# Hybrid attention and recurrence layer on one Trainium2 core: the value projections taken first, from x without its norm, and the rest of the order around them

## Chip, core and metric

One core of one Trainium2 chip runs the kernel. The metric is the device time of one execution in microseconds (us). The kernel before was run three times: 492.39, 494.06 and 495.75 us, a median of 494.06 us.

## The reference, cut to what matters

One layer, 512 tokens, model width 1024, all in float32:

```python
xn = rmsnorm(h, norm_gain)
aq, ak, av, ag, bq, bf, bi, bg, gate_a, gate_b = split(xn @ w_in)
qa, ka, va = rmsnorm(heads(aq)), rmsnorm(heads(ak)), heads(av)      # 8 heads x 64
ya = (causal_attention(qa, ka, va, rel_bias) * silu(ag)) @ w_up_a
log_f, kb, qb, vb = gates(bf), (1 - lb) * sigmoid(-bf), silu(bq), bi # 4 heads x 128
yb = (rmsnorm(hgrn2(qb, kb, vb, log_f)) * silu(bg)) @ w_up_b
h = h + (sigmoid(gate_a) * ya + sigmoid(gate_b) * yb) @ w_out
out = h + (p @ w_ple) * sigmoid(h @ w_ple_gate)
```

The norm of x is one factor per token (1/rms) and one per channel (the gain). A projection whose output has a token on each partition can therefore be made from x times the gain alone, and the factor per token multiplied in when the result is taken out of PSUM.

## The kernel before, in words

Every float32 product is made of three matmuls on rounded parts: high x high, high x low, low x high. A weight tile comes by DMA into a raw tile (two buffers), ScalarE (ACT) rounds it to its high part `wh`, VectorE (DVE) subtracts to get the low part `wl` (`split`, L181; three buffers of each). `weight` (L238) asks for the tile two places ahead, so that `wh` and `wl` of tile i+2 are made while TensorE (PE) works on tile i; the slot that they need is that of tile i-1, and comes free when the last matmul on that tile is done.

PE's order is written by hand: a manual schedule runs instructions in the order in which the code emits them. The main line emits projections and, after every three matmuls or so, adds their length to a clock of its own (`tick`, L120). Side jobs (generators given to `spawn`, L99) say how long they want to wait and emit their next piece once that clock has reached the time. The order on the other engines comes from the scheduler, which places instructions by readiness in its own timeline and by priority: code under `tc.high_priority` is preferred.

The main line: `bi` (the recurrence's values) from `gh`, `gl` (x times the gain, L282); the sum of squares of x on ACT, GpSimd (POOL) and DVE while that runs (`x_squares`, L292); `x_normalise` (L307) makes 1/rms with two small matmuls `mp` and `mt` and then `xh`, `xl`, the normalised x. From these come `bf` and `bq` of the four recurrence heads (each followed by `hgrn_gates`, L422), then `aq`, `ak`, `av`, and then the list `ORDER` (L43): the silu projections `bg` and `ag`, the merge gates `gb` and `ga`, and the up-projections `ub` of the recurrence between them. After the list come `ua`, `h` (w_out) and `g` (w_ple_gate, with `pe` for w_ple).

Side jobs: `recurrence` (L590) for four heads, whose pieces `HP` = 3.2 us apart make ratio tiles `hx` on DVE and ACT, score matmuls `lpb` and `lpa`, then `hktp`, `hds`, `hop` and `hms`; it starts `H0` = 23.85 us after the first head's gates. `qk_norm` (L601) for q and k ends in the transposes `qtp`, `ktp`. `attention` (L631) has 16 steps (4 head pairs, 4 query blocks): scores `s` on PE, then on DVE and ACT the softmax `p` (add the bias and find the maximum, L649; exp, L651; reciprocal; scale, L653), then transposes `pt` on PE, and `o` (times the values) once per head pair. A step is `AP` = 6.0 us of the main line's clock: 0.7 of it lies between scores and transposes of the same step.

`hgrn_gates` of a head: ACT makes `ha` = log(1 + exp(-|bf|)) in three passes and `hu` in two, DVE makes `hu`, `ha`, `hk`, POOL adds `ha` and `hu` (L435), and DVE scans that sum in four pieces (L439); then come the sigmoid of `bq` and the product with it.

Of the kernel before, what the change touches and what calls it, by code (L numbers as in the profile page):

```python
# [15 lines left out]
OP = mybir.AluOpType  # L16
# [14 lines left out]
HP = 3.2  # L31
AP = 6.0
H0 = 23.85
XN = 1.45
# [8 lines left out]
ORDER = [("bg", 0), ("ag", 0), ("bg", 1), ("ag", 1), ("gb", 0), ("gb", 1), ("bg", 2), ("ag", 2), ("gb", 2), ("gb", 3),  # L43
         ("bg", 3), ("ag", 3)] + [("gb", i) for i in range(4, 8)] + [("ga", 4), ("ga", 5), ("ga", 6), ("ub", 0), ("ub", 1)]
ORDER += [("ga", 7), ("ub", 2), ("ub", 3), ("ga", 0), ("ub", 4), ("ub", 5), ("ga", 1), ("ub", 6), ("ub", 7), ("ga", 2),
          ("ga", 3)]
# [7 lines left out]
def hybrid_layer_kernel(  # L54
# [136 lines left out]
    def w_sequence():  # L191
        for kp in range(4):
            wseq.append((w_tok[2, kp], 2, 512))
        for i in range(GH):
            wseq.append((w_tr[i], KD, 128))
            wseq.append((w_tr[4 + i], KD, 128))
        for g in (0, 1):
            for kp in range(4):
                wseq.append((w_tok[g, kp], 2, 512))
        for kp in range(4):  # L200
            wseq.append((w_tok[3, kp], 2, 512))
# [100 lines left out]
    def x_norm():
        with tc.high_priority():
            x_normalise()
        yield 0.0

    def x_normalise():  # L307
        ssum = ssums[1]
        V.tensor_tensor(ssum, ssum, ssums[0], op=OP.add)
# [28 lines left out]
        rsqrt(rt, tt, mt[:, 0:NT])  # L338

# [22 lines left out]
    def proj_tr(i, name):  # L362
        ws = weight(w_tr[i])
        ps = bank("mm", name)
        mm3(ps, ws[0], ws[1], xh, xl, KD)
        return ps

    def proj_pair(ids, names):

        ws = [weight(w_tr[i]) for i in ids]  # L370
        ps = [bank("mm", n) for n in names]
        for k in range(KD):
            for p, (wh, wl) in zip(ps, ws):
                for j, (a, b) in enumerate(((wh, xh), (wh, xl), (wl, xh))):
                    PE.matmul(p, a[:, k, :], b[k], start=(k == 0 and j == 0), stop=(k == KD - 1 and j == 2))
            tick(1.362)
        return ps
# [253 lines left out]
    def attention(qn, kn, va, sags, res):  # L631
# [57 lines left out]

        steps = [(hp, qb) for hp in range(HPAIRS) for qb in range(NT)]  # L690
# [31 lines left out]
    def start(kp):  # L722
        with tc.high_priority():
# [9 lines left out]
            elif kp == 1:  # L733
# [15 lines left out]
    lower_bound()
    spawn(recurrence(vb, sbgs, yb))  # L750
    for i in range(GH):
        if i == 0:
            f_, q_ = proj_pair((0, 4), ("bf0", "bq0"))
        else:
            f_ = proj_tr(i, f"bf{i}")
            q_ = proj_tr(4 + i, f"bq{i}")
# [151 lines left out]
```

## Time and profile before

| what | us |
|---|---|
| median of three runs | 494.06 |
| the profiled execution, device time | 494.47 |
| its span, first to last instruction | 492.5 |
| PE busy | 476.8 (97%) |
| DVE busy | 302.0 (61%) |
| ACT busy | 261.8 (53%) |
| POOL busy | 37.4 (8%) |

How to read the rows below: a timeline row is start, length, engine, line, operation, output <- inputs, shapes and count; behind it in brackets the idle time of the engine just before, and what ended it. Matmuls overlap: a 512-column matmul shows 0.39 us, but the next starts 0.227 us after it, so that an idle time of PE in brackets is some 0.16 us less than the time that PE lost there.

### The profile page before, as it was taken

Reading aid. Unit: us, or ns where it says so; the run is one execution under the profiler, and the core shown is the slowest. Engines: PE = TensorE matmul, PEld = TensorE weight load, DVE = VectorE, ACT = ScalarE, POOL = GpSimd, SP = SyncE. Lnnn points to the kernel's source line nnn. Section 1 sums busy time; section 2 is a strip of 40 time slices with the busy share of each in tenths; the row PEclk is TensorE's granted clock in tenths of the full one; section 3 lists DMA queues with packets and bytes.
Section 4 is the critical chain, followed back from the end, with each engine's and each line's share of the span. In section 5 each row is a group of like instructions: output and inputs, shape, how many; then the busy total and the mean of one; then the engine's idle time right before and its main releaser. Section 6 shows DMA issues by size and latency. Waiting matters only on the chain.

```text
span 492.5 us, 7947 instructions
## 1 busy us (share of the span) xinstructions
PE 476.8 (97%) x3160; PEld 387.2 (79%) x3160; DVE 302.0 (61%) x592; ACT 261.8 (53%) x458; POOL 37.4 (8%) x46
## 2 busy tenths in 40 slices
PE   7889999999999997999999999999999999999996
PEld 6668887888788776787777787888888888888885
DVE  3897886668985888359666544333327955534332
ACT  6665867535545777468685656644334533233111
POOL 3230221050401000010001000000000000000000
PEclk9999999999999999999999999999999999999999
DMA  8331332521231323113212222423323554323211
GB/s 276 128 120 66 110 128 88 149 87 45 63 94 60 91 82 115 58 44 94 79 44 99 75 64 91 130 81 95 119 64 87 192 191 129 108 85 128 87 43 43
DMA packets 17797, 48.41 MB, mean 98 GB/s; under 512 B 2232, under 2 KB 2616, under 8 KB 17760
## 3 DMA queue, kind: packets, MB, share of 16 engines
q1 hardware_dynamic: 17616, 47.83, 30.1%
q8 instruction: 24, 0.39, 0.3%
q0 software_dynamic: 144, 0.09, 0.1%
q14 instruction: 13, 0.11, 0.1%
HBM read 45.79 MB, written 2.12 MB: 97 GB/s over the span
## 4 chain that ended last, share of the span: by engine, by line
PE 88%; DVE 6%; DMA 2%; issue 2%; ACT 1%; SPq 0%; DVEq 0%; ACTq 0%
PE ga L251 9%; PE g L251 9%; PE h L251 9%; PE gb L251 8%; PE bg L251 5%; PE aq L399 5%; PE ak L399 4%; PE ub L251 4%; PE ua L251 4%; PE av L399 4%; PE ag L251 4%; PE bq L251 3%; PE bf L251 3%; PE pe L251 2%; PE s L642 2%; PE o L679 2%
## 5 line engine op out<-in xcount | busy, mean ns | idle before, releaser
L183 DVE TENSOR_TENSOR wl<-wf,wh 128x1024 fp32r<-128x1024 f32 (+1 forms) x81 | 92.3, 1141 | 85.8 <-ACT wh L182 85.5
L182 ACT ACTIVATE wh<-wf 128x1024 fp32r<-128x1024 f32 (+1 forms) x81 | 78.0, 963 | 122.9 <-PE ga L251 26.6
L251 PE MATMUL gb<-xh,wh 128*128 128x512 f32 x64 | 27.5, 429 | 0.0
L251 PE MATMUL g<-hl,wh 128*128 128x512 f32 (+1 forms) x72 | 26.3, 365 | 0.0
L251 PE MATMUL g<-hh,wl 128*128 128x512 f32 (+1 forms) x72 | 26.3, 365 | 0.0
L251 PE MATMUL g<-hh,wh 128*128 128x512 f32 (+1 forms) x72 | 26.3, 365 | 0.0
L651 ACT ACTIVATE p<-p,ps 128x128 f32<-128x128 f32 (+3 forms) x32 | 17.8, 556 | 15.0 <-DVE ps L649 14.9
L251 PE MATMUL gb<-xh,wl 128*128 128x512 f32 x64 | 25.4, 397 | 0.1
L251 PE MATMUL gb<-xl,wh 128*128 128x512 f32 x64 | 25.5, 398 | 0.0
L251 PE MATMUL ga<-xh,wh 128*128 128x512 f32 x64 | 25.3, 396 | 0.0
L251 PE MATMUL ga<-xl,wh 128*128 128x512 f32 x64 | 24.9, 389 | 0.0
L251 PE MATMUL ga<-xh,wl 128*128 128x512 f32 x64 | 24.9, 389 | 0.0
L251 PE MATMUL h<-ml,wh 128*128 128x512 f32 x64 | 24.9, 389 | 0.0
L251 PE MATMUL h<-mh,wl 128*128 128x512 f32 x64 | 24.9, 389 | 0.0
L251 PE MATMUL h<-mh,wh 128*128 128x512 f32 x64 | 24.9, 389 | 0.0
L649 DVE CUSTOM_DVE_ANT_0 p<-s,bias 128x128 f32<-128x128 f32 (+3 forms) x32 | 14.7, 488 | 15.7 <-PE s L642 15.7
L461 ACT ACTIVATE hx<-hx 128x512 f32<-128x512 f32 x24 | 14.9, 630 | 7.6 <-DVE hx L460 7.3
L530 POOL COPY sc<-s 32x128 f32<-32x128 f32 x16 | 8.7, 544 | 128.5 <-DVE s L481 127.9
L663 PE MATMUL pt<-ident,p 128*128 128x128 f32 x80 | 12.4, 287 | 5.0 <-DVE p L653 5.0
L667 ACT ACTIVATE ptS<-pt 128x128 f32<-128x128 f32 (+3 forms) x32 | 12.8, 435 | 7.3 <-PE pt L663 7.1
L806 DVE TENSOR_TENSOR hf<-h,xres 128x512 f32<-128x512 f32 x8 | 5.5, 692 | 18.1 <-PE h L251 18.1
L663 PEld LDWEIGHTS pt<-ident,p 128*128 128x128 f32 x80 | 9.9, 145 | 7.9 <-DVE p L653 6.3
(339 smaller groups left out, 1273.3 us busy)
## 6 DMA issues: line engine op xcount, KB each, us to landing
wf<-in_w_tr_dram SPq DMA_DIRECT2D x32, 512.0 KB, 3.3
wf<-in_w_tok_dram SPq DMA_DIRECT2D x15, 512.0 KB, 3.4
wf<-in_w_up_dram SPq DMA_DIRECT2D x16, 256.0 KB, 2.6
wf<-in_w_o_dram SPq DMA_DIRECT2D x8, 512.0 KB, 3.5
wf<-in_w_g_dram SPq DMA_DIRECT2D x8, 512.0 KB, 3.4
xr<-in_xT_dram SPq DMA_DIRECT2D x8, 256.0 KB, 6.1
bias<-ed SPq DMA_DIRECT2D x8, 256.0 KB, 3.4
xres<-in_xT_dram SPq DMA_DIRECT2D x8, 256.0 KB, 2.9
```

The lines of the kernel that those rows point to most:

```text
L182: A.activation(hi, src, AF.Copy)
L183: V.tensor_tensor(lo, src, hi.bitcast(F32), op=OP.subtract)
L251: PE.matmul(ps, a[:, k, :], b[k], start=(n == 0), stop=(n == tot - 1))
L399: PE.matmul(banks[t], a[:, s_], b[:, kk, :], start=(k == 0 and i == 0), stop=(k == KD - 1 and i == 2))
L461: A.activation(x, x, AF.Exp)
L530: G.tensor_copy(sc[s_, :, s_], s32[s_])
L642: PE.matmul(sps[j][:, :nk], a[js, qs], b[js, :nk], start=(i == 0), stop=(i == 2))
L649: V.tensor_tensor_reduce(pr[:, :nk], sp[:, :nk], T[j][:, nk - 1::-1], -1.0, 3e38, OP.add, OP.min, st[:, 0:1])
L651: A.activation(pr[:, :nk], pr[:, :nk], AF.Exp, bias=st[:, 0:1], scale=-1.0, accum_out=st[:, 1:2])
L663: PE.transpose(tp[:, kb * 128:kb * 128 + 128], prs[j][:, kb * 128:kb * 128 + 128], ident)
L667: A.activation(pt, tp[:, :nk], AF.Copy)
L679: PE.matmul(o[64 * j:64 * j + 64, qs], va[kb][:, h0:h0 + 64], pts[qb][j][:, kb * 128:kb * 128 + 128], start=(kb == 0), stop=(kb == qb))
```

## The change

`bi` is still first, from `gh` and `gl`. Behind it comes `av` (attention's values), which moves from the fourth place to the second and is also made from `gh` and `gl`; its evacuation from PSUM multiplies by 1/rms (`rt`). `bi` leaves PSUM without the factor, and four added ACT passes multiply it in later. The sum of squares becomes one chain: eight squares on ACT, seven sums on DVE, none on POOL. `mp` and `mt` stand in the middle of `av`. The paired loop for the first head's `bf` and `bq` is gone. After that first head come `aq` and `ak`, and only then the heads 1 to 3. Attention waits, when it is emitted, for q and k, and starts among the projections of those heads. The spacings change: `HP` 3.2 to 4.2, `AP` 6.0 to 9.6, `H0` 23.85 to 8.0, `XN` 1.45 to 1.0. In `ORDER` all eight `ub` stand at the end.

```diff
-HP = 3.2
-AP = 6.0
-H0 = 23.85
-XN = 1.45
+HP = 4.2
+AP = 9.6
+H0 = 8.0
+XN = 1.0
...
-ORDER = [("bg", 0), ("ag", 0), ("bg", 1), ("ag", 1), ("gb", 0), ("gb", 1), ("bg", 2), ("ag", 2), ("gb", 2), ("gb", 3),
...
+         ("ga", 5), ("ga", 6), ("ga", 7)] + [("ub", i) for i in range(KD)]
...
-    def x_squares(k0, k1):
-        E = G if k0 == 0 else V
...
+    def x_squares():
+        A.activation(ssum, xr[0], AF.Square)
+        for k in range(1, KD):
             t = unit("H", f"xsq{k}")
             A.activation(t, xr[k], AF.Square)
-            E.tensor_tensor(ssum, ssum, t, op=OP.add)
-        ssums.append(ssum)
+            V.tensor_tensor(ssum, ssum, t, op=OP.add)
 
     def x_norm():
-        with tc.high_priority():
+        x_squares()
+        yield XN
+        with tc.high_priority(offset=AHEAD):
             x_normalise()
-        yield 0.0
...
         rsqrt(rt, tt, mt[:, 0:NT])
+        for t in range(NT):
+            A.activation(vb[t], vb[t], AF.Copy, scale=rt[:, t:t + 1])
...
+        while not {"q", "k"} <= done:
+            yield lambda: {"q", "k"} <= done
...
-    bi = proj_tok(2, "bi", gh, gl, start)
-    vb = values(bi, "bi", rt)
+
+    vb = values(proj_tok(2, "bi", gh, gl, start), "bi")
     lower_bound()
+    spawn(x_norm())
+    va = values(proj_tok(3, "av", gh, gl), "av", rt)
     spawn(recurrence(vb, sbgs, yb))
...
+    head(0)
+    spawn(qk_norm("q", proj_tok(0, "aq", xh, xl), qgain[:, 0:1], qn))
     spawn(bias_rows())
-    spawn(qk_norm("q", proj_tok(0, "aq", xh, xl), qgain[:, 0:1], qn))
     spawn(qk_norm("k", proj_tok(1, "ak", xh, xl), kgain, kn))
-    va = values(proj_tok(3, "av", xh, xl), "av")
-    spawn(attention(qn, kn, va, sags, ya), 2.0)
+    spawn(attention(qn, kn, va, sags, ya))
+    for i in range(1, GH):
+        head(i)
```

First place: PE, the end of the projection `bi`. Before, the first head follows at once, from the normalised parts `xh` and `xl` (L375 is the paired loop):

```order
L399 MATMUL bi_116<-wh_211,gh_243 128x512
L399 MATMUL bi_116<-wh_211,gl_244 128x512
L399 MATMUL bi_116<-wl_212,gh_243 128x512
L375 MATMUL bf_413<-xh_297,wh_260 128x512
L375 MATMUL bf_413<-xl_298,wh_260 128x512
L375 MATMUL bf_413<-xh_297,wl_261 128x512
```

Now `av` follows, from `gh` and `gl`, and the two small matmuls of the norm stand behind its ninth matmul:

```order
L383 MATMUL bi_117<-wl_202,gh_233 128x512
L383 MATMUL av_314<-wh_239,gh_120 128x512
L383 MATMUL av_314<-wh_239,gl_121 128x512
L383 MATMUL av_314<-wl_240,gh_120 128x512
L383 MATMUL av_314<-wh_239,gh_128 128x512
L383 MATMUL av_314<-wh_239,gl_129 128x512
L383 MATMUL av_314<-wl_240,gh_128 128x512
L383 MATMUL av_314<-wh_269,gh_183 128x512
L383 MATMUL av_314<-wh_269,gl_184 128x512
L383 MATMUL av_314<-wl_270,gh_183 128x512
L304 MATMUL mp<-ssum,onesd 128x512
L307 MATMUL mt<-onesd,ssum 128x1 x4
```

What moved: the 96 matmuls of `av` now lie between `bi` and the first instruction that needs `xh`, which is `bf` of head 0.

Second place: DVE, around attention's first softmax (head pair 0, query block 0, two heads). `ISA` rows are the pass that adds the bias and takes the maximum, each with a row that reads its accumulator. Before, two weight tiles and one split of the recurrence stand ahead of it:

```order
L183 TENSOR_TENSOR wl_1490<-wf_1487,wh_1489 128x1024
L183 TENSOR_TENSOR wl_1678<-wf_1675,wh_1677 128x1024
L183 TENSOR_TENSOR htl_1664<-ht_1661,hth_1663 128x512
L649 ISA p_1703,ps_1704<-s_1695,bias_1691 128x128
L649 ISA ps_1704 128x1
L649 ISA p_1709,ps_1710<-s_1696,bias_1693 128x128
L649 ISA ps_1710 128x1
L652 RECIPROCAL ps_1704<-ps_1704 128x1
L653 TENSOR_SCALAR p_1703<-p_1703,ps_1704 128x128
L652 RECIPROCAL ps_1710<-ps_1710 128x1
L653 TENSOR_SCALAR p_1709<-p_1709,ps_1710 128x128
```

Now the gates of head 2 (`hu_1429`, `ha_1425`, `hk_1434`, all from `bf_1290`) stand ahead of it, with the end of k's transposes (`kl`) and of head 0's output (`ho`):

```order
L182 TENSOR_TENSOR wl_1354<-wf_1351,wh_1353 128x1024
L264 TENSOR_TENSOR hy_1234<-hy_1234,ht_1235 128x512
L412 TENSOR_SCALAR hu_1429<-bf_1290 128x512
L186 SCALAR_TENSOR_TENSOR kl_1136<-ktp_1344,sm,kh_1132 128x512
L415 SCALAR_TENSOR_TENSOR ha_1425<-bf_1290,ha_1425 128x512
L561 SCALAR_TENSOR_TENSOR ho_1233<-hop_1225,sm,hy_1234 128x512
L448 TENSOR_TENSOR hx_1_1412<-hu_1267 128x256
L417 TENSOR_TENSOR hk_1434<-ha_1425,bf_1290 128x512
L633 ISA p_1382,ps_1383<-s_1374,bias_1370 128x128
```

Behind it, still on DVE, the scan of head 2 (L423, which reads POOL's sum) stands ahead of the scaling of both softmax tiles:

```order
L443 TENSOR_TENSOR hx_16_1491<-hu_1267 128x16x16
L444 TENSOR_TENSOR hx_16_1491<-hu_1267 128x16x16
L451 TENSOR_TENSOR hx_1_1412<-ha_1263,hx_1_1412 128x256
L636 RECIPROCAL ps_1383<-ps_1383 128x1
L423 SCALAR_TENSOR_TENSOR hu_1429<-onec,ha_1425 128x128 x2
L636 RECIPROCAL ps_1389<-ps_1389 128x1
L637 TENSOR_SCALAR p_1382<-p_1382,ps_1383 128x128
L423 SCALAR_TENSOR_TENSOR hu_1429<-onec,ha_1425 128x128 x2
L637 TENSOR_SCALAR p_1388<-p_1388,ps_1389 128x128
```

What moved: on PE these scores stand six matmuls into `bq` of head 2, that is six matmuls behind the end of its `bf`, and the transposes that wait for both softmax tiles stand 18 matmuls behind the scores.

## Rows read from the trace of the kernel before

**Rows 1.** The page: busy time of PE, share of the span, instructions
```profile
PE 476.8 (97%) x3160; PEld 387.2 (79%) x3160; DVE 302.0 (61%) x592; ACT 261.8 (53%) x458; POOL 37.4 (8%) x46
```
**Rows 2.** Busy time by stretch (PE, PEld, DVE, ACT, POOL, granted clock), a late stretch
```profile
340.00:360.00 20.00, 20.00 (x90) 16.57 (x89) 8.34 (x10) 8.54 (x12) 0.00 (x0) 1.00 0.33 95
```
**Rows 3.** Timeline of PE, the first 36 us: matmuls that waited, and the norm's
```profile
12.70 0.39 PE L399 MATMUL bi<-wh,gl 128*128 128x512 f32 x1
14.25 0.50 PE L399 MATMUL bi<-wl,gh 128*128 128x512 f32 x1 [1.17 <-DVE wl L183]
...
20.34 0.50 PE L399 MATMUL bi<-wl,gh 128*128 128x512 f32 x1 [0.36 <-DVE wl L183]
...
22.21 1.13 PE L311 MATMUL mp<-ssum,onesd 128*128 128x512 f32 x2
...
35.02 0.50 PE L375 MATMUL bf<-xl,wh 128*128 128x512 f32 x1 [1.68 <-DVE xl L183]
```
**Rows 4.** Timelines of POOL and DVE, the same stretch
```profile
10.44 4.90 POOL L299 TENSOR_TENSOR ssum<-ssum,xsq 128x512 f32<-128x512 f32 x3 [6.31 <-ACT xsq L298]
...
11.96 2.24 DVE L183 TENSOR_TENSOR wl<-wf,wh 128x1024 fp32r<-128x1024 f32 x1 [1.92 <-ACT wh L182]
14.12 2.44 DVE L187 SCALAR_TENSOR_TENSOR gl<-xr,sm,gh 128x512 fp32r<-128x512 f32 x2
```
**Rows 5.** Timeline of PE, 130 to 280 us, where it waited longest
```profile
133.41 0.51 PE L399 MATMUL av<-wl,xh 128*128 128x512 f32 x1 [0.22 <-DVE wl L183]
...
175.41 0.44 PE L663 MATMUL pt<-ident,p 128*128 128x128 f32 x2 [0.79 <-DVE p L653]
...
192.30 0.39 PE L251 MATMUL gb<-xh,wl 128*128 128x512 f32 x1
195.28 1.81 PE L663 MATMUL pt<-ident,p 128*128 128x128 f32 x8 [2.60 <-DVE p L653]
...
235.18 1.09 PE L663 MATMUL pt<-ident,p 128*128 128x128 f32 x8 [1.63 <-DVE p L653]
...
276.26 0.50 PE L574 MATMUL hms<-htl,ones 128*128 128x512 f32 x1 [0.30 <-DVE htl L183]
```
**Rows 6.** Busy time by stretch (columns as in rows 2), behind two waits
```profile
196.00:197.00 1.00, 1.00 (x7) 1.00 (x6) 0.42 (x1) 0.60 (x1) 0.00 (x0) 0.50 0.86 299
...
198.00:199.00 1.00, 1.00 (x4) 0.76 (x4) 0.00 (x0) 0.00 (x0) 0.00 (x0) 0.54 0.00 0
199.00:200.00 1.00, 1.00 (x6) 0.55 (x5) 0.00 (x0) 0.00 (x0) 0.00 (x0) 1.00 0.00 0
...
235.00:236.00 1.00, 0.82 (x7) 0.82 (x8) 1.00 (x4) 0.86 (x3) 0.00 (x0) 1.00 0.38 156
```
**Rows 7.** Timeline of DVE, what it did while PE waited at 193 us
```profile
193.61 1.22 DVE L183 TENSOR_TENSOR wl<-wf,wh 128x1024 fp32r<-128x1024 f32 x1
194.75 0.48 DVE L653 TENSOR_SCALAR p<-p,ps 128x512 f32<-128x512 f32 x1
```
**Rows 8.** Head 2's gates: chain of waits (PE), then timelines of ACT, DVE, POOL
```profile
56.89 5.44 PE bf L251 x24
...
62.14 1.07 ACT L182 ACTIVATE wh<-wf 128x1024 fp32r<-128x1024 f32 x1
...
65.83 0.71 ACT L426 ACTIVATE ha<-ha,onec 128x512 f32<-128x512 f32 x1
...
68.61 0.68 DVE L433 TENSOR_TENSOR hk<-ha,bf 128x512 f32<-128x512 f32 x1
...
69.90 1.68 POOL L435 TENSOR_TENSOR ha<-ha,hu 128x512 f32<-128x512 f32 x1 [7.37 <-ACT hu L430]
...
71.61 1.37 DVE L439 TENSOR_TENSOR_SCAN hu<-onec,ha 128x128 f32<-128x128 f32 x4 [1.19 <-POOL ha L435]
```
**Rows 9.** Groups by line: busy us, mean ns of one, idle before
```profile
L183 DVE TENSOR_TENSOR wl<-wf,wh 128x1024 fp32r<-128x1024 f32 (+1 forms) x81 | 92.3, 1141 | 85.8 <-ACT wh L182 85.5
L649 DVE CUSTOM_DVE_ANT_0 p<-s,bias 128x128 f32<-128x128 f32 (+3 forms) x32 | 14.7, 488 | 15.7 <-PE s L642 15.7
...
L435 POOL TENSOR_TENSOR ha<-ha,hu 128x512 f32<-128x512 f32 x4 | 6.4, 1602 | 41.0 <-DVE hk L433 33.6 <-ACT hu L430 7.4
```

More of the change, by code (lines that the diff above doesn't have):

```diff
@@ L41 @@
 ONPOOL = (2, 4, 6)
-ORDER = [("bg", 0), ("ag", 0), ("bg", 1), ("ag", 1), ("gb", 0), ("gb", 1), ("bg", 2), ("ag", 2), ("gb", 2), ("gb", 3),
-         ("bg", 3), ("ag", 3)] + [("gb", i) for i in range(4, 8)] + [("ga", 4), ("ga", 5), ("ga", 6), ("ub", 0), ("ub", 1)]
-ORDER += [("ga", 7), ("ub", 2), ("ub", 3), ("ga", 0), ("ub", 4), ("ub", 5), ("ga", 1), ("ub", 6), ("ub", 7), ("ga", 2),
-          ("ga", 3)]
+ORDER = [("ag", 0), ("bg", 0), ("bg", 1), ("ag", 1), ("gb", 0), ("gb", 1), ("gb", 2), ("bg", 2), ("ag", 2), ("gb", 3), ("gb", 4),
+         ("gb", 5), ("bg", 3), ("ag", 3), ("ga", 0), ("ga", 1), ("gb", 6), ("gb", 7), ("ga", 4), ("ga", 2), ("ga", 3),
+         ("ga", 5), ("ga", 6), ("ga", 7)] + [("ub", i) for i in range(KD)]
 AHEAD = 150
@@ L191, in w_sequence @@
     def w_sequence():
-        for kp in range(4):
-            wseq.append((w_tok[2, kp], 2, 512))
-        for i in range(GH):
+        for g in (2, 3, None, 0, 1):
+            if g is None:
+                wseq.extend([(w_tr[0], KD, 128), (w_tr[4], KD, 128)])
+            else:
+                wseq.extend((w_tok[g, kp], 2, 512) for kp in range(4))
+        for i in range(1, GH):
             wseq.append((w_tr[i], KD, 128))
             wseq.append((w_tr[4 + i], KD, 128))
[L197 to L201, printed above, removed]
         for kind, i in ORDER:
@@ L288, in x_gain @@
             gl.append(l_)
-    ssums = []
-    def x_squares(k0, k1):
-        E = G if k0 == 0 else V
-        ssum = unit("H", f"ssum{k0}")
-        A.activation(ssum, xr[k0], AF.Square)
-        for k in range(k0 + 1, k1):
+    ssum = unit("H", "ssum")
+    def x_squares():
+        A.activation(ssum, xr[0], AF.Square)
+        for k in range(1, KD):
             t = unit("H", f"xsq{k}")
             A.activation(t, xr[k], AF.Square)
-            E.tensor_tensor(ssum, ssum, t, op=OP.add)
-        ssums.append(ssum)
+            V.tensor_tensor(ssum, ssum, t, op=OP.add)
     def x_norm():
-        with tc.high_priority():
+        x_squares()
+        yield XN
+        with tc.high_priority(offset=AHEAD):
             x_normalise()
-        yield 0.0
     def x_normalise():
-        ssum = ssums[1]
-        V.tensor_tensor(ssum, ssum, ssums[0], op=OP.add)
         mp = bank("g", "mp")
@@ L365, in proj_tr @@
         mm3(ps, ws[0], ws[1], xh, xl, KD)
[L366 to L376, printed above, removed]
         return ps
@@ L736, in start @@
                 x_gain(4, 6)
-                x_squares(0, 4)
             elif kp == 2:
@@ L740, in start @@
                 x_gain(6, 8)
-                x_squares(4, 8)
-                spawn(x_norm(), XN)
             else:
@@ L746, in hybrid_layer_kernel, with head @@
     ya, yb, qn, kn, sags, sbgs = [], [], [], [], [], []
-    bi = proj_tok(2, "bi", gh, gl, start)
-    vb = values(bi, "bi", rt)
+    vb = values(proj_tok(2, "bi", gh, gl, start), "bi")
     lower_bound()
+    spawn(x_norm())
+    va = values(proj_tok(3, "av", gh, gl), "av", rt)
     spawn(recurrence(vb, sbgs, yb))
[L751 to L756, printed above, removed]
+    def head(i):
+        f_ = proj_tr(i, f"bf{i}")
+        q_ = proj_tr(4 + i, f"bq{i}")
         hgrn_gates(i, f_, q_)
+    head(0)
+    spawn(qk_norm("q", proj_tok(0, "aq", xh, xl), qgain[:, 0:1], qn))
     spawn(bias_rows())
-    spawn(qk_norm("q", proj_tok(0, "aq", xh, xl), qgain[:, 0:1], qn))
     spawn(qk_norm("k", proj_tok(1, "ak", xh, xl), kgain, kn))
-    va = values(proj_tok(3, "av", xh, xl), "av")
-    spawn(attention(qn, kn, va, sags, ya), 2.0)
+    spawn(attention(qn, kn, va, sags, ya))
+    for i in range(1, GH):
+        head(i)
     def up(i, n, ys, name):
```

## The prediction, made before the changed kernel ran

> **What bounds the kernel now.** I read the page first: PE is busy 97% of the span, DVE 61%, ACT 53% [rows 1]. So only time that PE lost can be won, and the question is where it lost any. The stretches late in the span show PE full with the granted clock at 1.00 [rows 2]: there 24 full matmuls follow in 5.44 us, 0.227 each [rows 8], and nothing can be won. Everything before is searched in PE's timeline for matmuls that started late. Each costs its bracket plus 0.16 us, because a matmul's row lasts 0.39 us and its successor starts after 0.227.
>
> In the first 36 us there are three: from 12.70 to 14.25, 1.55 less 0.23 = 1.32; at 20.34, 0.36 + 0.16 = 0.52; at 35.02, 1.68 + 0.16 = 1.84, where the first head's `bf` waits for the normalised x [rows 3]. Together **3.7 us**. The first has a cause beside it: the low part of that weight tile took DVE 2.24 us, against 1.14 on average [rows 4, 9], and the two passes after it 2.44 together, while POOL ran its sums of squares for 4.90 us.
>
> From 130 to 280 us there are five: 0.38 (`av` on a weight's low part), 0.95, 2.75 (192.30 to 195.28, less 0.23) and 1.79 on softmax tiles, 0.46 at `hms` [rows 5]. The third has an aftermath: the granted clock stood at 0.50, that is 1.2 GHz, until about 198.6 [rows 6], so that some 3.3 us from 195.28 on ran at half speed, 1.65 lost. The wait at 235.18 left the clock at 1.00. Sum **8.0 us**. What DVE did meanwhile shows the cause: it runs in program order, and a weight tile of 1.22 us stood between the reciprocal and the scaling that PE waited for [rows 7].
>
> So 11.7 us can be removed in all. The profiled execution took 494.47 us, 0.4 over the median; I subtract from its time and take the 0.4 off at the end.
>
> **The change, part by part.**
>
> *`av` behind `bi`, from x without its norm.* 96 matmuls, 21.8 us, now stand between `bi` and the first `xh`. In before, `mp` ran at 22.21 and the first low part came at 35.02, 12.8 us later [rows 3]; now `mp` stands nine matmuls into `av`, with 87 matmuls or 19.7 us behind it, and the later parts are wanted later still. The 1.84 goes. If the cover fell short, the same 1.84 would come back.
>
> *Squares and sums.* POOL's three sums are gone, so the tile that took 2.24 should take 1.14, and the first wait falls by 1.1 to 0.2. DVE has seven sums instead of four, three more at 0.68 or 2.0 us, but saves 1.0 on the two passes that took 2.44 [rows 4]. That decides the second wait: between 0 and 0.52 + 1.0 = 1.5. I take 0.3, near the low end, since PE loses its pause for `mp` in the middle of `bi` but the sums of the last tiles stand behind the passes that PE needs. Left over here: 0.5 (0.2 to 1.7).
>
> *Four added ACT passes for `rt`, the lost paired loop.* ACT is idle half of the span [rows 1], and the passes lie under `av`. Nothing; without that cover four steps of 0.6, 2.4.
>
> *`av` in two halves of weight pairs.* Its third pair of tiles comes when the first slots free, as at 133.41 in before, which lost 0.38 [rows 5]. I put 0.4 (0 to 1).
>
> *Heads 1 to 3 behind `ak`, attention among them.* This is where a new wait comes, and the order shows it. Take the end of head 2's `bf` as zero. PE does six matmuls of `bq` (1.36) and the first scores (I put 0.6, under the 1.36 of six full matmuls): their end is 2.0. 18 matmuls later, at 6.1, it wants both softmax tiles to transpose them. On DVE the maximum of the first tile stands behind `hk` of head 2, which hangs on ACT: a weight tile that starts when the slot comes free at the end of `bf` (1.07), then three passes of `ha` and one of k, at about 0.6 a step, 3.4 in all. DVE then does `ha`, `ho`, `hx` and `hk`, 2.2: `hk` ends at 5.6. POOL's sum takes 1.6 [rows 9], so the scan can start at 7.3, and half of it stands ahead of the first tile's scaling, the rest ahead of the second's: 8.3 for the first tile, 9.1 for the second. PE waits 9.1 - 6.1 = **3.0**, most of it (2.2) in one piece. That is the low end. The high end is the same chain in before: `bf` ended at 62.33, `hk` at 69.29, the scan started at 71.61 [rows 8], which is 7.0 and 9.3 after it, with other recurrence passes in between; then the second tile is done at 11.1 and PE waits 5.0. I take 3.7, nearer to the low end, because in the new order fewer such passes stand inside the chain.
>
> *The clock behind it.* One idle piece of 2.60 us was followed by the half clock, one of 1.63 was not [rows 5, 6]. Mine is 2.2 to 4.2, nearer to the first. I take the 1.7 that it cost there; the bounds are 0 and 1.7.
>
> *`hms` of head 0.* Its low part on DVE stands behind the scan of head 1, and that behind POOL's sum: a weight tile (1.07 and 1.14), three passes, 1.6, 1.37 and the split, some 7.6 us after the end of `bf` of head 1, against 5.44 for the next 24 matmuls and the `hop` pieces between. So at most 2.2; at least 0.46 as in before [rows 5]. I take 1.0.
>
> *Wider spacing of attention and recurrence.* Scores and their transposes stood 4.2 us of the main line apart (0.7 of 6.0), now 6.7. The lateness in before was 0.95, 2.75 and 1.79 us; 2.5 more us of matmuls cover all three but for 0.25, and DVE's passes, which are the same in number, now lie under some 12 us of PE's work from score to score instead of 8. The 0.46 at the later heads' `hms` I leave in, 0.5.
>
> *Up-projections last.* `o` of the last pair stands in the fifth `ub`, 45 matmuls or 10.2 us ahead of `ua`; the chain behind `o` is one product and two splits, about 2.5. Hidden. Each `ub` is 2.7 us of PE against two short passes each on DVE and ACT; the late stretch has both engines under half busy [rows 2]. Without that cover PE would lose up to 2.5 once.
>
> **The sum.** Removed 3.7 + 8.0 = 11.7; left over or new 0.5 + 0.4 + 3.7 + 1.7 + 1.0 + 0.5 = 7.8. Net 3.9: 494.47 - 3.9 = 490.6, less the 0.4: **490.2 us**.
>
> **The rivals.**
>
> *The clock stays up behind the new wait.* For it: the wait at 235.18, 1.63 us, left it alone; against it, 2.60 did not. 490.2 - 1.7 = 488.5.
>
> *The first softmax is not late.* If the scheduler's order suits the chip better than my chain, 3.7 and 1.7 drop out: 484.8. For it: before the change DVE was waiting for the scores more often than the reverse, 15.7 us in all [rows 9]. Against it: the chain ACT, DVE, POOL, DVE is in the order, whatever the speed.
>
> *POOL's sum holds DVE off.* In rows 4 a DVE pass with two SBUF inputs took 1.1 us more while POOL ran. The recurrence passes that now stand between the maximum and the scaling of the first softmax tiles run beside POOL's sum of head 2, and would be held off by up to its 1.6: 490.2 + 1.6 = 491.8. The Trainium skill says the same in "SBUF — State Buffer", section "Who interferes with whom": a VectorE instruction with two SBUF inputs and a GpSimd instruction that reads SBUF exclude each other for a whole instruction, whichever started first. By that rule, which rows 4 bear out with 2.24 against 1.14, the change gains at the start and pays here.
>
> *The early gain does not come.* All eight squares stand ahead of the third weight tile on ACT. If x arrives late, they hold it and the 3.2 won at the start are gone: 493.4. Against it: in before seven of them stood there, with 0.52 lost.
>
> *Slower.* The gates of head 3 and the recurrence of head 1 follow on DVE at once. If each of the four score steps of the first head pair waits as the one at 195.28 did, 2.75 + 1.65, three more of them cost 13.2: 503.4. It takes DVE some 5 us more work in each of these steps than PE has matmuls; counting the passes between two scores in the new order, at 0.6 for 512 columns and 1.14 for a weight tile, I find 0.8 more in one step and 3 to 7 less in the others.
>
> **How the numbers follow.** Forecast 0.36; clock stays 0.20; first softmax in time 0.14; POOL 0.12; no early gain 0.12; slower 0.06. A change of 1% is 4.9 us, about what a measurement of this kernel can tell from none. Faster by over 1% means under 489.1: the second and third case and, by the low ends of its terms, 0.08 of the forecast, 0.42. Slower means over 499.0: 0.06. The rest, 0.52, is within 1%. The range 484.8 to 493.5 leaves out the slow case and about half each of the two outermost others, under 0.2. The forecast's own range is 489 to 492.
>
> **What would show it.** Right: `bf` of head 0 starts without a wait about 53 us into the span (35.02 - 1.84 - 0.23, where it was due before, less 1.4 and plus 21.8); the tile that took 2.24 takes about 1.2; no wait over 0.5 at `pt` from the second score step on; one wait of 3 to 4 us at the first `pt`, on DVE's softmax, and the clock at 0.50 for some 3 us behind it. Wrong: that wait is missing, or several like it; PE waiting at the third weight tile of `bi`; PE waiting at `ua` for attention's end.

## The result, and the profile after

| kernel | median us | lowest to highest | profiled execution | its span |
|---|---|---|---|---|
| before | 494.06 | 492.21 to 495.75 (5 runs) | 494.47 | 492.5 |
| changed | 490.07 | 488.94 to 491.69 (5 runs) | 488.94 | 487.1 |

The ratio is 0.9917, with a 95% interval of 0.9894 to 0.9939: 4.0 us off, within the 1% that the prediction counted as no change, and 0.1 from its 490.2. The profiled executions differ by more, 5.5 us, because that of the changed kernel is its fastest. Where the prediction placed the losses is another matter, and the profile shows it.

The start, in PE's timeline (as [rows 3]; start us, us, engine, line, operation, tiles, shapes, and in brackets the idle time and what ended it), and one row of DVE's (as [rows 4]):

```profile
12.66 0.39 PE L383 MATMUL bi<-wh,gl 128*128 128x512 f32 x1
12.96 0.50 PE L383 MATMUL bi<-wl,gh 128*128 128x512 f32 x1
...
18.35 0.39 PE L383 MATMUL bi<-wh,gl 128*128 128x512 f32 x1
18.75 0.50 PE L383 MATMUL bi<-wl,gh 128*128 128x512 f32 x1
...
44.16 0.50 PE L383 MATMUL av<-wl,gh 128*128 128x512 f32 x1 [0.19 <-DVE wl L182]
...
53.35 0.39 PE L248 MATMUL bf<-xh,wh 128*128 128x512 f32 x1
```

```profile
11.68 1.23 DVE L182 TENSOR_TENSOR wl<-wf,wh 128x1024 fp32r<-128x1024 f32 x1
```

Full matmuls start 0.227 us apart, so the first two places cost 0.30 - 0.23 = 0.07 and 0.40 - 0.23 = 0.17, and the third 0.19 + 0.16 = 0.35. The waits of 1.17 and 0.36 of [rows 3] are gone, and so is that of 1.68: `bf` follows `av` without a pause. The low part that took 2.24 us beside POOL takes 1.23.

The middle, PE's timeline at every wait over 0.2 us between 120 and 260 us, and the first transposes of the softmax (`pt`), which did not wait (as [rows 5]):

```profile
128.78 0.50 PE L558 MATMUL hms<-htl,ones 128*128 128x512 f32 x1 [1.16 <-DVE htl L182]
...
136.66 0.66 PE L608 MATMUL ktp<-ident,kr 128*128 128x128 f32 x4 [0.50 <-DVE kl L186]
...
138.63 0.33 PE L626 MATMUL s<-kh,qh 64*128 64x128 f32 x1
140.64 0.33 PE L626 MATMUL s<-kh,qh 64*128 64x128 f32 x1 [1.69 <-DVE kl L186]
...
146.93 0.38 PE L647 MATMUL pt<-ident,p 128*128 128x128 f32 x2
...
254.94 0.50 PE L558 MATMUL hms<-htl,ones 128*128 128x512 f32 x1 [0.28 <-DVE htl L182]
```

PE does not wait at the first `pt`. It waits one step earlier, at the second of the two first score tiles `s`, until DVE is done with the last of the four passes that make the low parts of k. DVE's timeline has these four passes `kl`, and what stood between the last two (as [rows 7]):

```profile
132.66 0.74 DVE L186 SCALAR_TENSOR_TENSOR kl<-ktp,sm,kh 128x512 fp32r<-128x512 f32 x1
...
135.85 0.75 DVE L186 SCALAR_TENSOR_TENSOR kl<-ktp,sm,kh 128x512 fp32r<-128x512 f32 x1
...
136.85 0.74 DVE L186 SCALAR_TENSOR_TENSOR kl<-ktp,sm,kh 128x512 fp32r<-128x512 f32 x1
137.51 1.22 DVE L182 TENSOR_TENSOR wl<-wf,wh 128x1024 fp32r<-128x1024 f32 x1
138.64 0.68 DVE L264 TENSOR_TENSOR hy<-hy,ht 128x512 f32<-128x512 f32 x1
139.24 0.69 DVE L412 TENSOR_SCALAR hu<-bf 128x512 f32<-128x512 f32 x1
139.84 0.74 DVE L186 SCALAR_TENSOR_TENSOR kl<-ktp,sm,kh 128x512 fp32r<-128x512 f32 x1
```

Between the third and the fourth `kl` stand a weight tile, a pass of head 0's output norm and the first gate pass of head 2.

What PE waits for is not an operand. The row that waits is `s<-kh,qh`, which reads no low part, and these scores are those of the first head pair, whose low part is that of the first `kl`, done at 133.40. It is a PSUM buffer: in kernel.py `bank("a", ...)` has two, and the transposes of k, the scores, the transposes of the softmax and `o` take turns in them. Each tile has to wait until the tile two places ahead of it has been read. The fourth transposes of k start at 136.66, 0.06 us after the second `kl` ends, and the second score tile at 140.64, 0.06 us after the fourth `kl` ends. In the run below with the spacing undone, four such starts in a row (136.75, 140.62, 142.88 and 145.47) come 0.05 or 0.06 us after the ends of its four `kl`. No run gave `a` a third buffer, so this rests on the kernel's text and these times.

Behind that wait the granted clock falls, as it did in [rows 6] (stretch, its length, busy us and count of PE, PEld, DVE, ACT and POOL, granted clock, DMA):

```profile
141.00:142.00 1.00, 1.00 (x6) 0.83 (x5) 1.00 (x3) 0.44 (x1) 0.00 (x0) 0.83 0.35 139
142.00:143.00 1.00, 1.00 (x4) 0.71 (x4) 1.00 (x5) 0.65 (x2) 0.08 (x1) 0.50 0.00 0
...
145.00:146.00 1.00, 1.00 (x5) 0.76 (x5) 1.00 (x6) 0.48 (x1) 0.00 (x0) 0.96 0.00 0
```

From 142 to 145 us it stands at 0.50, that is 1.2 GHz. With 0.17 and 0.04 for the edges and 1.5 between, 1.7 us are lost. The three waits at `pt` of [rows 5] have no counterpart. The late stretch is as full as in [rows 2].

### The profile page after: what moved, and what is told of

Its sections match the earlier page's. It is cut to its first block, busy times and chain, and to the rows that moved or that the text cites. A ratio compares the mean times of both kernels' runs of the same rounds, so it can differ in the third digit from the quotient of the medians.

```text
span 487.1 us, 7939 instructions
## 1 busy us (share of the span) xinstructions
PE 475.9 (98%) x3160; PEld 387.3 (80%) x3160; DVE 301.2 (62%) x595; ACT 266.5 (55%) x462; POOL 30.3 (6%) x43
## 4 chain that ended last, share of the span: by engine, by line
PE 92%; DVE 4%; ACT 1%; DMA 1%; POOL 1%; issue 1%; SPq 0%; DVEq 0%; POOLq 0%
PE ga L248 9%; PE gb L248 9%; PE g L248 9%; PE h L248 9%; PE bi L383 5%; PE ak L383 5%; PE ag L248 5%; PE ub L248 5%; PE ua L248 4%; PE aq L383 4%; PE bg L248 4%; PE av L383 4%; PE bq L248 3%; PE bf L248 3%; PE pe L248 2%; PE s L626 2%
## 5 line engine op out<-in xcount | busy, mean ns | idle before, releaser
L182 DVE TENSOR_TENSOR wl<-wf,wh 128x1024 fp32r<-128x1024 f32 (+1 forms) x81 | 89.2, 1103 | 75.4 <-ACT wh L181 74.9
L248 PE MATMUL gb<-xh,wh 128*128 128x512 f32 x64 | 26.3, 410 | 0.0
L514 POOL COPY sc<-s 32x128 f32<-32x128 f32 x16 | 7.0, 436 | 142.8 <-DVE s L465 63.1
L248 PEld LDWEIGHTS g<-hh,wh 128*128 128x128 f32 x72 | 13.6, 189 | 2.2
L248 PEld LDWEIGHTS g<-hh,wl 128*128 128x128 f32 x72 | 13.6, 189 | 2.2
```

Of the source, the lines that this page charges most:

```text
L182: V.tensor_tensor(lo, src, hi.bitcast(F32), op=OP.subtract)
L248: PE.matmul(ps, a[:, k, :], b[k], start=(n == 0), stop=(n == tot - 1))
L514: G.tensor_copy(sc[s_, :, s_], s32[s_])
```

## The experiments

Each kernel was timed in five rounds (4 to 12 executions) beside the kernel before; a ratio is against the runs of before made with it, whose medians were 493.60 to 493.90.

### Which part of the change does what

**The new start alone**, on the kernel before:

```diff
-    bi = proj_tok(2, "bi", gh, gl, start)
-    vb = values(bi, "bi", rt)
+    vb = values(proj_tok(2, "bi", gh, gl, start), "bi")
     lower_bound()
+    spawn(x_norm())
+    va = values(proj_tok(3, "av", gh, gl), "av", rt)
...
-    va = values(proj_tok(3, "av", xh, xl), "av")
     spawn(attention(qn, kn, va, sags, ya), 2.0)
```

> The kernel before with the new start alone: av directly behind bi from the x without its norm, rt multiplied in afterwards, all seven sums of squares on DVE; the four heads, aq, ak, the order of the later blocks and the spacing of attention and recurrence stay as before. Theory (the gain of the start and the gain of the later stages are separate sums, and the start carries the larger one): PE lost 4.5 and 2.4 us in the first two stretches of 20 us before and 3.1 and 0.1 after, so 3.8 us go, 0.35 comes back as av waits for a weight's low part; the waits at the softmax tiles stay: about 490.6 where before has 494.1, and the first bf without a wait. Rival (av was the cover between ak and the first scores; without it attention starts while the gates of the heads still fill DVE): the waits at the softmax tiles grow by more than 2 us and the time is 493 or more.

Measured: 486.24 us, ratio 0.9852 (0.9830 to 0.9874). That is 7.5 off, twice the theory's 3.5 and 3.8 better than the whole change. PE's timeline holds these waits over 0.3 us behind the start:

```profile
183.79 0.50 PE L571 MATMUL hms<-htl,ones 128*128 128x512 f32 x1 [0.56 <-DVE htl L183]
...
244.27 0.66 PE L660 MATMUL pt<-ident,p 128*128 128x128 f32 x4 [0.58 <-DVE p L650]
245.66 0.66 PE L660 MATMUL pt<-ident,p 128*128 128x128 f32 x4 [0.73 <-DVE p L650]
```

They cost 0.8, 0.7 and 0.9, 2.5 together, where [rows 5] held 8.0. The granted clock stays at 1.00 behind them. So the waits at the softmax went mostly with the new start, at the old spacing. Both theory and rival had them stay or grow.

**The rest of the change alone**: `av` behind `bi`, but from the normalised x, with the norm's old place and POOL's sums.

```diff
-    vb = values(proj_tok(2, "bi", gh, gl, start), "bi")
+    vb = values(proj_tok(2, "bi", gh, gl, start), "bi", rt)
     lower_bound()
-    spawn(x_norm())
-    va = values(proj_tok(3, "av", gh, gl), "av", rt)
+    va = values(proj_tok(3, "av", xh, xl), "av")
```

> The changed kernel with the old start: av still stands directly behind bi, but takes the normalised x, and the sums of squares are shared with POOL as before. Everything behind av is as in the changed kernel. Theory (start and rest are separate sums): the three early waits come back, 3.7 us, and the time is about 490.1 + 3.5 = 493.6, close to before; the waits at hms, at the k transposes and at the first scores are those of the changed kernel, 1.3 + 0.7 + 2.0, with the half clock behind them. Rival (the later stages carry the gain, the start only little): 491 or less.

Measured: 493.48, ratio 1.0003 (0.9987 to 1.0018), as the theory had it. Without the new start nothing is gained. The early waits came back, with 0.25 and 0.77 more in `av` behind the 1.66 on the low parts of x. One row differs from what was expected, the clock; this is the same wait as in the changed kernel, and the stretch behind it:

```profile
145.53 0.32 PE L628 MATMUL s<-kh,qh 64*128 64x128 f32 x1 [1.69 <-DVE kl L186]
```

```profile
146.00:147.00 1.00, 1.00 (x5) 0.86 (x5) 1.00 (x4) 0.33 (x1) 0.00 (x0) 1.00 0.19 74
```

The same 1.69 us of idle time left the clock at 1.00 here and brought it to 0.50 there. But with the clock up PE reached the first transposes of the softmax sooner, and waited there:

```profile
151.06 0.33 PE L649 MATMUL pt<-ident,p 128*128 128x128 f32 x1 [0.69 <-DVE p L639]
151.88 0.33 PE L649 MATMUL pt<-ident,p 128*128 128x128 f32 x1 [0.50 <-DVE p L639]
```

With 0.16 for each that is 1.5 us, about what the half clock cost in the changed kernel.

**The new start and the order of the later blocks**: up-projections last, heads and spacing as before.

```diff
-ORDER += [("ga", 7), ("ub", 2), ("ub", 3), ("ga", 0), ("ub", 4), ("ub", 5), ("ga", 1), ("ub", 6), ("ub", 7), ("ga", 2),
+         ("ga", 5), ("ga", 6), ("ga", 7)] + [("ub", i) for i in range(KD)]
```

> The new start alone with one thing more: the order of the later blocks as in the change, with the eight up-projections last. The four heads stand ahead of aq and ak and the spacing is that of before. Theory (the up-projections last are hidden, as the prediction has it, and the order of the blocks is not what costs): within 1.5 us of the new start alone, 485.0 to 487.7. Rival (the order of the blocks is the part of the change that gives the gain of the start back): 489 or more, with waits at the softmax tiles among blocks that hang on them.

Measured: 485.95, ratio 0.9856 (0.9832 to 0.9879), the same as the start alone. The order of the blocks costs nothing and brings nothing, as the prediction had it.

**The spacing undone**: the changed kernel with the old one.

```diff
-HP = 4.2
-AP = 9.6
+HP = 3.2
+AP = 6.0
```

> The changed kernel with the spacing of before for attention and recurrence (6.0 and 3.2 us of the main line instead of 9.6 and 4.2); start, order of the heads and order of the blocks stay as changed. Theory of the prediction (the wider spacing is what took the waits of 0.95, 2.75 and 1.79 us at the softmax tiles away): with PE's matmuls between two score steps cut from some 12 us to 8, waits at the transposes of the softmax come back, 5.5 us and up to 1.65 of half clock: 494 to 497. Rival (those waits hung on where av stood, since they were gone with the new start alone; the spacing does little): 488.5 to 491, with no wait over 1 us at a transpose behind the first score step.

Measured: 493.91, ratio 1.0006 (0.9987 to 1.0024). The time is near the theory's, but its place is not. Most is lost where k is transposed and scored, and one wait of 1 us stands at a transpose of the softmax:

```profile
140.62 0.66 PE L608 MATMUL ktp<-ident,kr 128*128 128x128 f32 x4 [1.82 <-DVE kl L186]
...
145.47 0.47 PE L626 MATMUL s<-kh,qh 64*128 64x128 f32 x1 [2.27 <-DVE kl L186]
...
248.41 0.55 PE L647 MATMUL pt<-ident,p 128*128 128x128 f32 x3 [1.04 <-DVE p L637]
```

The first two are the wait for a PSUM buffer again. Behind the second the clock stood at 0.50 until nearly 152 us, some 6 us.

These four and the changed kernel are steps of one ladder. New start: -7.5. Order of the blocks: -0.3. Heads 1 to 3 behind `ak`, with head 0 unpaired, its recurrence earlier and attention's start 2.0 us earlier (485.95 to 493.91): **+8.0**. Wider spacing (493.91 to 490.07): **-3.8**. By the ratios the four are -7.3, +0.2, +7.4 and -4.4 us, so a step is known to about 1 us. The heads were not moved without the other edits in that step, so the 8.0 belongs to those together.

The steps hang on their order. With the rest alone first (493.71 to 493.48), the rest brings 0.2 and the new start on top of it 3.4. The place of `av`, directly behind `bi`, is in the runs of both the start alone and the rest alone; no run moves `av` and nothing else.

### The wait at the first scores

**Scores later**: attention begins 2.5 us of the main line after k's last transpose.

```diff
             yield lambda: {"q", "k"} <= done
+        yield 2.5
         steps = [(hp, qb) for hp in range(HPAIRS) for qb in range(NT)]
```

> The changed kernel with one line more: attention starts 2.5 us of the main line after the last k transpose instead of at once, so that eleven or twelve full matmuls stand ahead of the first scores. Theory (the first scores wait 1.69 us because the low part of k, 0.74 us on DVE, stands behind seven recurrence and gate passes; and this idle piece is what lets the clock fall): the wait at the first scores goes, 2.0 us, and the half clock behind it, 1.6 us: about 486.5, with the granted clock at 1.00 from 135 to 150 us. Rival 1 (the clock falls on account of the matmuls of 64 rows or the transposes there, not of the idle piece): the wait goes but the clock falls again, about 488.1. Rival 2 (the wait moves on to the first transposes of the softmax, which the prediction feared): a wait of 2 us or more there, 490 or more.

Measured: 489.04, ratio 0.9908 (0.9889 to 0.9927). Rival 2's mechanism holds, though its 490 or more was not reached: the wait at the scores is gone and a longer one stands at the first `pt`, with the half clock behind it. PE's timeline, DVE's, and one stretch:

```profile
148.47 0.69 PE L647 MATMUL pt<-ident,p 128*128 128x128 f32 x2 [2.38 <-DVE p L637]
```

```profile
144.95 1.36 DVE L423 TENSOR_TENSOR_SCAN hu<-onec,ha 128x128 f32<-128x128 f32 x4
146.23 1.20 DVE L182 TENSOR_TENSOR wl<-wf,wh 128x1024 fp32r<-128x1024 f32 x1
...
148.14 0.47 DVE L637 TENSOR_SCALAR p<-p,ps 128x128 f32<-128x128 f32 x2
```

```profile
149.00:150.00 1.00, 1.00 (x4) 0.81 (x4) 0.20 (x1) 0.47 (x2) 0.00 (x0) 0.50 0.92 344
```

This is the wait that the prediction forecast, at its place and behind its scan of head 2, with a weight tile on top.

**Scores and first transposes later**: the edit above, and

```diff
+            if n == 1:
+                yield 3.0
             if 1 <= n <= len(steps):
                 pts[n - 1] = transposed(*steps[n - 1], prs.pop(n - 1))
```

> The changed kernel with the first scores 2.5 us of the main line later, as before, and the first two transposes of the softmax 3.0 us later on top; nothing else. Theory (one lateness of DVE, about 2.4 us, stands behind the wait at the first scores, and behind the wait at the first transposes that took its place; the half clock follows any such idle piece): both waits go and the clock stays at 1.00, so 489.0 - 2.5 - 1.6 = 484.9, with PE losing nothing between 140 and 155 us. Rival 1 (the lateness moves on once more, to the second score step): a wait of 1 us or more there and 487 to 489. Rival 2 (the clock falls all the same): no wait, but some 3 us at 0.50 and about 486.5.

Measured: 487.37, ratio 0.9884 (0.9863 to 0.9906). Both waits are gone (the scores at 142.46 have none either) and the clock stays up:

```profile
150.58 0.38 PE L647 MATMUL pt<-ident,p 128*128 128x128 f32 x2
```

```profile
148.00:151.00 3.00, 3.00 (x16) 2.47 (x15) 2.51 (x9) 2.77 (x5) 0.00 (x0) 1.00 0.40 122
```

The theory's mechanism is shown. Its size is not: 1.7 us came of the 4.1 awaited. Waits of 0.42 us at the second `pt` step (164 us) and 0.35 at `hms` (190 us) are new; with 0.16 for each they cost 1.1. The profiled execution also lost time at its start, where its matmuls came 0.43 us apart until 10.3 us: it reached the `hms` of head 0 at 129.90, where the run with later scores had 128.64. Behind that place it saved 2.5 us (spans 487.2 and 486.0, and the 1.26), against 4.1 - 1.1 = 3.0.

**All four waits at once**: the two edits above, k's transposes 2.4 us apart instead of 1.3, and the sum ahead of the scan on DVE.

```diff
-        G.tensor_tensor(a, a, um, op=OP.add)
+        V.tensor_tensor(a, a, um, op=OP.add)
...
-            yield 1.3
+            yield 1.3 if name == "q" else 2.4
```

> The changed kernel with four small edits: first scores 2.5 us and first transposes 3.0 us later, as before; the k transposes 2.4 us apart instead of 1.3; the sum ahead of the gates' scan on DVE. Theory (what the change still loses beside the two waits that the later scores took away is the wait at hms behind POOL's sum, 1.3 us, and that at the k transposes, 0.7): both go, 487.4 - 1.5 = 485.9. Rival (the lateness of DVE in this stretch is one sum, and moves to the next wait): 487 or more with a new wait of 1 us at the first score steps.

Measured: 485.70, ratio 0.9833 (0.9811 to 0.9854), the theory's number. The wait at the k transposes went, and those at 164 and 190 us. That at `hms` fell only from 1.16 to 0.99:

```profile
129.63 0.50 PE L558 MATMUL hms<-htl,ones 128*128 128x512 f32 x1 [0.99 <-DVE htl L182]
```

```profile
128.45 0.53 DVE L505 TENSOR_TENSOR hkd<-hu 128x384 f32<-128x384 f32 x1
128.90 0.68 DVE L182 TENSOR_TENSOR htl<-ht,hth 128x512 fp32r<-128x512 f32 x1
```

DVE no longer waits for POOL, but a pass that stood behind `htl` now stands ahead of it. So the changed order of the heads can be had at about the time of the new start alone, with all these edits.

### POOL at the start

**Three sums back on POOL**, in the changed kernel:

```diff
+        for s_, k0, E in ((ssum, 0, G), (ssum4, 4, V)):
...
-            V.tensor_tensor(ssum, ssum, t, op=OP.add)
+                E.tensor_tensor(s_, s_, t, op=OP.add)
```

> The changed kernel with three of the seven sums of squares given back to POOL; av still from x without its norm. Theory (POOL held the DVE passes off at the start): a weight's low part beside POOL's sums takes some 2.2 us again instead of 1.23, and PE waits 1.0 to 1.5 us for it: about 491.3. Rival (the wait at 14.25 us came from the squares' place on ACT, or av covers it now): no more than 0.3 above the changed kernel, 490.1 to 490.4, and the low part at 1.2 us.

Measured: 490.14, ratio 0.9924 (0.9908 to 0.9940), so no cost that can be told from the changed kernel's 490.07. But the passes are held off as in [rows 4]. POOL's, DVE's and PE's timelines:

```profile
10.26 4.91 POOL L296 TENSOR_TENSOR ssum<-ssum,xsq 128x512 f32<-128x512 f32 x3 [6.14 <-ACT xsq L295]
```

```profile
11.77 2.24 DVE L182 TENSOR_TENSOR wl<-wf,wh 128x1024 fp32r<-128x1024 f32 x1 [1.91 <-ACT wh L181]
```

```profile
9.66 0.63 PE L386 MATMUL bi<-wh,gh 128*128 128x512 f32 x1
10.08 0.60 PE L386 MATMUL bi<-wh,gl 128*128 128x512 f32 x1
...
14.07 0.50 PE L386 MATMUL bi<-wl,gh 128*128 128x512 f32 x1
```

The tile took 2.24 again, yet PE did not wait for it, since its matmuls had started 0.43 us apart until 10.5 us and it came to the tile late. So that POOL held DVE off is shown, by 1.0 us; what this costs the kernel is not settled. In the run with the rest alone, whose matmuls were 0.23 us apart from 7.2 us on, PE waited 1.13 at this place, but there the squares stand elsewhere too.

### Where the waits at the softmax had gone

**Attention later in the new start alone**, by 6.0 us, so that it meets the recurrence of head 2 as in the kernel before:

```diff
             yield lambda: {"q", "k"} <= done
+        yield 6.0
         steps = [(hp, qb) for hp in range(HPAIRS) for qb in range(NT)]
```

> The new start alone with attention begun 6.0 us of the main line later, so that the first scores stand to the recurrence of head 2 as they did in the kernel before (its row of block products just ahead of the fourth score step instead of behind it). Theory (the waits of 0.95, 2.75 and 1.79 us at the softmax tiles, which went with the new start although it doesn't touch them, hung on which recurrence passes of head 2 stood beside which score step): waits of 2 us or more at transposes come back, with the half clock behind one of them: 489 to 492. Rival (they went because all gates of the heads and the value projection's tiles are out of the way by then, whatever the phase): no wait over 1 us there, 486 to 487.

Measured: 488.69, ratio 0.9888 (0.9869 to 0.9907), between the two. The profiled execution is the fastest, 487.30, with a mean granted clock of 0.999; the other five had 0.991 to 0.996, so the half clock that the theory had may stand in those, at a place that no trace shows. The waits below are of the fastest. The counterpart of the wait of 2.60 at 195.28 in [rows 5], at the fourth step of the first head pair, is 0.33; the second pair's waits grew. PE's timeline, and DVE's at the first of them:

```profile
209.80 0.66 PE L660 MATMUL pt<-ident,p 128*128 128x128 f32 x4 [0.33 <-DVE p L650]
...
248.09 0.65 PE L660 MATMUL pt<-ident,p 128*128 128x128 f32 x4 [1.05 <-DVE p L650]
250.15 0.66 PE L660 MATMUL pt<-ident,p 128*128 128x128 f32 x4 [1.41 <-DVE p L650]
```

```profile
209.27 0.48 DVE L650 TENSOR_SCALAR p<-p,ps 128x512 f32<-128x512 f32 x1
...
210.26 1.22 DVE L183 TENSOR_TENSOR wl<-wf,wh 128x1024 fp32r<-128x1024 f32 x1
```

Here the scaling comes ahead of the weight tile; in [rows 7] it came behind it, and ahead of that tile stood the low part of head 1's gated output, in DVE's timeline of the kernel before:

```profile
192.48 0.69 DVE L183 TENSOR_TENSOR ybl<-bg1s,ybh 128x512 fp32r<-128x512 f32 x1
```

So at the first pair the place of the recurrence does not decide alone; which other passes are due beside the same score step counts too. That the move of `av` changed these is an argument from the order of the blocks, not shown by a run of its own. What lies in the way at the second pair stays open.

**Spacing 7.2 us in the new start alone**:

```diff
-AP = 6.0
+AP = 7.2
```

> The new start alone with attention spaced a little wider, 7.2 us of the main line instead of 6.0; all else as before. The new start alone has two waits left at softmax tiles, 0.74 and 0.90 us at 243 us. Theory (a wider spacing covers a lateness of under 1 us, and attention still ends ahead of the up-projections that need it): those two go, 1.5 us, and the time is 484.7. Rival 1 (the recurrence keeps its pace, so each score step meets other recurrence passes and new waits come): 486 to 488. Rival 2 (attention ends too late and PE waits at the first up-projection): 488 or more with a wait there.

Measured: 485.12, ratio 0.9837 (0.9813 to 0.9860). No `pt` waits over 0.3 us any more; the 1.1 us is near the 1.5 expected.

**The same with the new order of blocks and the sum on DVE** (edits as above):

> The new start, the order of blocks of the change, attention spaced 7.2 us, and the sum ahead of the gates' scan on DVE instead of POOL. Theory (the sum on POOL takes 1.3 to 1.6 us there and back and DVE 0.68; the low part at hms stands behind the scan, so the wait of 0.63 at hms that the run with 7.2 us had shrinks to nothing): 485.1 - 0.6 = 484.5. Rival (four passes more on DVE are 2.7 us, which come out again at a softmax tile): 485.5 to 487.

Measured: **484.29**, ratio 0.9806 (0.9786 to 0.9826), the fastest here, 5.8 us under the changed kernel. But the wait at `hms` is what it was, for it stands behind a weight tile and not behind a scan:

```profile
184.51 0.50 PE L570 MATMUL hms<-htl,ones 128*128 128x512 f32 x1 [0.63 <-DVE htl L182]
```

```profile
182.63 1.23 DVE L182 TENSOR_TENSOR wl<-wf,wh 128x1024 fp32r<-128x1024 f32 x1 [3.91 <-ACT wh L181]
```

The expected mechanism fell, and the intervals of this kernel and the last overlap.

**Spacing 7.8 us, new order, sum on POOL**:

> The new start, the order of blocks of the change with the up-projections last, attention spaced 7.8 us; the sum on POOL. Theory (7.2 us already covers every lateness at the softmax tiles, more spacing has nothing left to win, and the last pair's output still stands nine matmuls ahead of the first up-projection that needs it): 485.0 to 485.6. Rival (attention ends too late): PE waits at the first up-projection of attention, 486 or more.

Measured: 484.77, ratio 0.9819 (0.9795 to 0.9844), 0.2 under the range expected. Its interval overlaps those of both runs with 7.2 us: nothing more to win, and no wait at the up-projections.

## Why the prediction came out right, and where it was wrong

The time was right, 490.07 for 490.2. Its terms, in us, against the rows of the changed kernel:

| term | predicted | measured |
|---|---|---|
| left of the waits in `bi` | 0.5 | 0.07 + 0.17 |
| `av` on a weight's low part | 0.4 | 0.35 |
| `hms` of head 0 | 1.0 | 1.16 + 0.16 = 1.3 |
| k transposes | not named | 0.50 + 0.16 = 0.7 |
| first scores | not named | 1.69 + 0.32 = 2.0 |
| first `pt` | 3.7 | 0 |
| half clock | 1.7 | 1.7 |
| later `hms` | 0.5 | 0.28 + 0.16 = 0.4 |
| sum | 7.8 | 6.7 |

Removed were 11.7 as forecast, so the rows make a net of 5.0, against 5.5 between the two profiled executions and 4.0 between the medians.

*The start* came as forecast in the rows: `bf` at 53.35 for "about 53", the tile at 1.23 for 1.2, the 1.84 covered by `av`. That POOL's sums alone were behind the first wait is not settled, as said above.

*The first `pt`* is the step that failed. The prediction counted from the end of head 2's `bf` and had PE at the softmax 6.1 us later, with nothing in the way but matmuls. It did not ask whether the buffers were free into which the last transposes of k and the scores are written. These hung on the `kl` passes, which stand in the same DVE queue as head 2's gates. DVE's chain itself was right. `bf` ended at 136.16, and the second softmax tile was done 10.8 us later, between the 9.1 and the 11.1 of the prediction:

```profile
146.67 0.26 DVE L637 TENSOR_SCALAR p<-p,ps 128x128 f32<-128x128 f32 x1
```

But PE was late by then, by 0.7 at the k transposes, 2.0 at the scores and 1.7 of half clock, and had nothing left to wait for. The run with the rest alone, with the clock up, had the same two waits and then 1.5 us at `pt`. The run with later scores put the wait where the prediction had it, 2.38 us where it gave 3.0 to 5.0; the run with both later took both away. One lateness was paid once. That is why the sum held although the place did not.

*The wider spacing* was credited with the 7.1 us of waits and half clock at the softmax. Of the 8.0 us in the middle, 5.5 went with the new start alone at the old spacing. What the spacing did was to give back 3.8 of the 8.0 that the move of the heads costs. The kernel before was not run with the wide spacing alone, so whether that would have taken the waits too stays open. By its own terms the prediction had the start at 3.7 - 0.5 - 0.4 = 2.8 and all the rest at a gain of 8.0 - 6.9 = 1.1. With the start put in last it is near: 3.4 and 0.2. With the start put in first it is far off: 7.5, and the rest a cost of 3.8. The difference is the waits at the softmax, which went with whichever part came first. That they were gone was forecast; that the wider spacing was not needed for it was not.

*Of the rivals*, "the first softmax is not late" did not come about: PE did not wait for it, but it was as late as forecast. "The clock stays up" is what the run with the rest alone shows, but not the gain of 1.7, since PE then waits at `pt`. One of the changed kernel's own five executions had a mean granted clock of 1.000 and took 490.07 us, in the middle of the others. "POOL's sum holds DVE off" was seen, in DVE's and POOL's timelines of the changed kernel:

```profile
143.11 1.37 DVE L443 TENSOR_TENSOR hx<-hu 128x256 f32<-128x256 f32 x1
144.40 0.41 DVE L444 TENSOR_TENSOR hx<-hu 128x256 f32<-128x256 f32 x1
```

```profile
142.92 1.28 POOL L419 TENSOR_TENSOR ha<-ha,hu 128x512 f32<-128x512 f32 x1 [16.18 <-DVE hk L417]
```

The first pass took 1.37 us beside POOL's sum, against 0.41 for its like just after it and 0.42 for the same line at 131.38. PE, late already, did not wait for it, so it cost nothing there. In the run with later scores it took 1.38 (at 142.98), and DVE had no pause from there to the scaling, so there it is part of the 2.38 that PE waited. The Trainium skill's "SBUF — State Buffer", section "Who interferes with whom", has a VectorE instruction with two SBUF inputs and a GpSimd instruction that reads SBUF exclude each other; these rows agree (1.37 against 0.41), and so does the run with POOL's sums (2.24 against 1.23). "The early gain does not come" and "slower" did not happen, though with the spacing undone the gain was gone.

## What to carry to other kernels

When work is moved under a full engine, follow for the first steps behind it not only the operand that looks latest, but also the buffer that each step writes: who has to empty it, and what stands ahead of that pass in its queue. A wait one step early hides the one behind it, and taking one away uncovers the other. Judge a compound change by a ladder of its parts, and climb it in more than one order; here the start was worth 7.5 us put in first and 3.4 put in last. Waits that hang on which passes happen to stand side by side can vanish with an edit far ahead of them, so credit them to an edit only after a run without it.

## What the hardware showed that was not expected

- The length of an idle piece of PE alone does not tell whether the granted clock falls. With pieces of 2.27, 2.38 and 2.60 us it fell to 0.50 about their end. Of the shorter ones it fell with 1.69 in the changed kernel and 1.68 with POOL's sums back, and did not with 1.63 [rows 5, 6], 1.69 in the run with the rest alone and 1.82 at 140.62 with the spacing undone. The same wait with the same waits of 1.16 and 0.50 ahead of it went both ways.
- It differs between executions of one kernel, too. Of the kernel before, 34 were timed in the first two sets of experiments. 16 had a mean granted clock of 1.000, with medians of 492.6 and 492.4 us in the two sets; the other 18 had 0.993 to 0.997, with 494.3 and 494.4. So the 1.65 of half clock that the prediction counted as removable is paid in some executions only.
- With POOL's sums back, PE's matmuls started 0.43 us apart from 5.65 to 10.5 us, though the granted clock reads 1.00 there; in the changed kernel it was 0.23 from 7.5 us on. 0.43 is the spacing where the clock reads 0.50 (142.12, 142.55, 142.97 in the changed kernel), that is 1.2 GHz, and that trace's record of the clock begins only at 10.53 us: the 1.00 ahead of it stands for no record. The run with both waits taken away, that with attention 6.0 us later and that with spacing 7.8 us begin like that, too, and in three others the record shows 0.50 from some 8 to 11 us. So a microsecond or two between profiled executions can come from the start alone.
